# A memory quarter and a gain vector moved from GpSimd's DMA queue to SyncE's, and later transposes tied to weight slices

## The chip, the cores and the metric

The kernel runs on one NeuronCore of a Trainium2 chip. Its time is the device time of one execution, in microseconds. Of the engines, TensorE (PE) multiplies matrices and transposes tiles by a product with the identity, VectorE (DVE) and ScalarE (ACT) do elementwise work, GpSimd (POOL) does small things, and SyncE (SP) issues transfers. Each engine runs its own list of instructions in order and waits on semaphores. Transfers go through 16 DMA engines; those that SyncE issues are queue q1 of the profile, those that GpSimd issues are q0.

## The reference

One decoder layer on x of 1024 tokens by 2048, and a memory of 256 tokens by 2048:

```python
h = rmsnorm(x, ln_g)
proj = h @ w_in                       # split into the inputs of three groups
# group A: gated MLP over chunks of 128; group B: gated DeltaNet, 8 heads
m = rmsnorm(mem, mem_norm_g)
mk, mv = split(m @ w_mem_kv)          # 2 x 512 columns
p = softmax(cq @ mk^T * 128**-0.5)    # group C: 4 heads, 256 memory tokens
out_c = (p @ mv) * silu(c_z)
y = rmsnorm(x + concat(A, B, C) @ w_out, final_g)
```

The change touches the loading of `mem` and `ln_g` for the first stage, the product `m @ w_mem_kv`, and the preparation of the first tiles of x beside it.

## The kernel before, in words

**Precision.** Every float32 operand of a large product is split into a high part (rounded to the fast format, cast by ScalarE) and a low part (the rest, by VectorE), and a product is three matmuls: high-high, high-low and low-high (`triple`). So each tile costs a cast on ScalarE and a subtraction on VectorE before TensorE can use it.

**The planner.** The body of the kernel does not issue instructions. Each call adds an operation to a `Plan`, with a class (`rank`), its data dependences and, inside `behind(op)`, one more dependence on `op`. `Plan.issue` then runs a list schedule over all engines, with a price for each operation, and emits the instructions in the order of the starts that it finds. The `behind` dependence exists in this planning alone: it moves an instruction in its engine's list, and no semaphore is made for it. Semaphores follow the data and the reuse of buffers. Because all orders come out of one schedule, a changed dependence can move instructions on every engine for some distance behind it.

**The memory K/V stage.** It opens the kernel. `w_mem_kv` comes as 16 slices of 128 rows by 1024 columns (`load_kv(k)`, 0.5 MB each; the first in two halves), into four buffers (two named wraw, two ut), so a slice can be issued when the low part of the slice four before it has been made. Memory has two row tiles of 128 tokens, held in tiles named kT and qT, each in four quarters of 512 columns (`load_mem(q)`: two transfers of 256 KB). `spread_mem(q)` transposes a quarter on TensorE, four 128x128 blocks per row tile into one of two PSUM banks, and splits it into gt (high) and inv (low). Quarter q serves slices 4q to 4q+3. For a slice, ScalarE makes whi (the weights times the norm's gain, cast), VectorE makes wlo, and TensorE adds 12 products of 256 columns into the four banks acc (the keys) and 6 of 512 columns into two banks dn (the values). There are two whi and two wlo buffers, so the cast of a slice waits for TensorE's last use two slices before. `kvmark[k]` is the last product of slice k.

**x beside it.** The first four tiles of x (128 tokens each, four pieces of 512 columns; tiles named vs, kd, then kT and qT again) are prepared inside this stage by `prep`: four squares with a sum on ScalarE (written to jk), the inverse root on GpSimd, a product with that and with ln_g on VectorE (ln_g lies in the four tiles gb, named zg, spread over the partitions by the transfer), a transpose on TensorE, a copy to tn and a cast to ahi on ScalarE, and alo on VectorE. tn is stored to h0d from SyncE. The scale of the memory's rows is found in the same way (squares of kT and qT) and applied at the stage's end, when VectorE empties acc into xr. The next stage, the large projection by `w_in`, then takes over the acc banks.

**Queues before.** SyncE's list opens with the first quarter, slices 0 to 3, then quarters 2 and 3 (counted from 0), then slices as buffers come free, mixed with the tiles of x. A semaphore is shared by every eighth transfer of SyncE, so a transfer waits until the one eight before it has landed. GpSimd issues the second quarter first of all (1.31 and 2.04 us) and the four spreads of ln_g at 3.71 us, although the code places these behind slice 2, as its list has nothing before them to wait for. In this kernel the transposes of the second quarter are planned with those of the first, and the third and fourth quarters are made available when slices 3 and 7 have been added.

Nearly every instruction bears line 295, where the planner calls it, so the tiles' names tell them apart.

Of the kernel before, what the change touches and what calls it, by code (L numbers as in the profile page):

```python
# [17 lines left out]
P = 128  # L18
# [4 lines left out]
HT = 512  # L23
# [37 lines left out]
class Plan:  # L61
# [27 lines left out]
    @contextmanager  # L89
    def rank(self, cls):  # L90
        old, self.cls = self.cls, cls
        yield
        self.cls = old

    @contextmanager
    def behind(self, op):
        old, self.gate = self.gate, op
        yield
        self.gate = old
# [199 lines left out]
def kernel(  # L299
# [21 lines left out]
    x, mem, w_in, out = x[0], mem[0], w_in[0], out[0]  # L321
# [7 lines left out]
    V, S, G, PE, Q = R.dve, R.act, R.pool, R.pe, R.sp  # L329
    rank, behind = R.rank, R.behind  # L330

    def C(shape, name, dt=F32):
        return sb.tile(list(shape), dt, name=name, tag=name)[:]
# [44 lines left out]
    def tok(ap):  # L378

        return ap.rearrange("p (t c) -> p t c", c=P)  # L380
# [59 lines left out]
    def split_to(hi, lo, src, eng):  # L440
        S.copy(hi, src)
        eng.tensor_tensor(out=lo, in0=src, in1=hi, op=ALU.subtract)
# [20 lines left out]
    def triple(a, l, r, start, stop, cls=9):  # L463

        mm(a, l[0], r[0], start, False, cls)
        mm(a, l[0], r[1], False, False, cls)
        return mm(a, l[1], r[0], False, stop, cls)
# [4 lines left out]
    def row_scale(xq):  # L472

        s = small()
        for c in range(4):
            S.activation(jk, xq[c], AF.Square, accum_out=s[:, c : c + 1])
        V.tensor_reduce(s[:, 4:5], s[:, 0:4], axis=AX.X, op=ALU.add)
        V.tensor_scalar(s[:, 4:5], s[:, 4:5], 1.0 / D, EPS, op0=ALU.mult, op1=ALU.add)
        rsqrt_to(s[:, 5:6], s[:, 4:5])
        return s[:, 5:6]  # L480


    def row_tiles(tag):
        if tag in ("inv", "gt", "ut"):
            return [b[:, i * HT : (i + 1) * HT] for b in (ring[tag](), ring[tag]()) for i in range(2)]
        return [ring[tag]() for _ in range(4)]

    gb = [ring["zg"]() for _ in range(4)]
    kvraw += [ring["ut"]() for _ in range(2)]
    mem_rows = [row_tiles("kT"), row_tiles("qT")]  # L490
    x_rows = {}

    def load_mem(q, queue=Q):
        for mt in range(2):
            queue.dma_start(mem_rows[mt][q], mem[mt * P : (mt + 1) * P, q * HT : (q + 1) * HT])

    def kv_parts(k):
        n = XW if k == 0 else 2 * XW
        return [slice(i, i + n) for i in range(0, 2 * XW, n)]

    def load_kv(k):
        for sl in kv_parts(k):
            Q.dma_start(kvraw[k % 4][:, sl], w_mem_kv[k * P : (k + 1) * P, sl])

    def load_x(tt, tag, after=(None,) * 4):
        x_rows[tt] = row_tiles(tag)
        for c in range(4):
            with behind(after[c] or R.gate):
                Q.dma_start(x_rows[tt][c], x[tt * P : (tt + 1) * P, c * HT : (c + 1) * HT])
# [4 lines left out]
    with rank(2):  # L514
        load_mem(0)
        S.dma_start(mrow, mem_norm_g[0].rearrange("(c p) -> c p", p=P))
        load_mem(1, G)
        for k in range(4):
            load_kv(k)
    with rank(3):  # L520
        load_mem(2)
        load_mem(3)
# [4 lines left out]
    def spare():  # L527
        turn["dn"] = 1 - turn["dn"]
        return flip[turn["dn"]]
# [6 lines left out]
    def spread_mem(q):  # L536
        h, l = (ring[t](F32R).rearrange("p (k n) -> p k n", k=4) for t in ("gt", "inv"))
        for mt in range(2):
            tp = spare()
            for k in range(4):  # L540
                PE.transpose(tp[:, k * P : (k + 1) * P], mem_rows[mt][q][:, k * P : (k + 1) * P], ident)
            sl = slice(mt * P, (mt + 1) * P)
            with rank(2):
                split_to(h[:, :, sl], l[:, :, sl], tok(tp), V)
        return h, l

    def prep(tt, put, bank):

        xq = x_rows[tt]
        r = row_scale(xq)  # L550
        for q in range(NQ):
            V.scalar_tensor_tensor(xq[q], xq[q], r, gb[q], op0=ALU.mult, op1=ALU.mult)
            tp = bank()
            for k in range(4):
                PE.transpose(tp[:, k * P : (k + 1) * P], xq[q][:, k * P : (k + 1) * P], ident)
            put(q, tok(tp))
# [6 lines left out]
    def put0(tt):  # L563
        def put(q, tp):
            t = tok(ring["tn"]())
            with rank(1):
                S.copy(t, tp)
            with rank(2):
                split_to(ahq[q][:, tt], alq[q][:, tt], t, V)
            with rank(6):  # L570
                Q.dma_start(h0_d[4 * q : 4 * q + 4, :, tt * P : (tt + 1) * P].rearrange("k p n -> p k n"), t)

        return put
# [2 lines left out]
    rm = []  # L576
    kvmark = []
    mhl = [spread_mem(0)]
    mhl.append(spread_mem(1))
    for k in range(KT):  # L580
        mh, ml = mhl[k // 4]
        if k >= 4:
            with rank(3):
                load_kv(k)
        hi, lo = kvhi[k % 2], kvlo[k % 2]
        with rank(2):
            for sl in kv_parts(k):
                raw = kvraw[k % 4][:, sl]
                S.activation(hi[:, sl], raw, AF.Copy, scale=gcol[:, k : k + 1])
                V.scalar_tensor_tensor(lo[:, sl], raw, gcol[:, k : k + 1], hi[:, sl], op0=ALU.mult, op1=ALU.subtract)  # L590
        kk = k % 4
        for h in range(NX):
            sl = slice(h * P, (h + 1) * P)
            triple(ka[h][:, :NMEM], (hi[:, sl], lo[:, sl]), (mh[:, kk], ml[:, kk]), k == 0, k == KT - 1)
        for mt in range(2):
            sl = slice(mt * P, (mt + 1) * P)
            triple(va[mt], (mh[:, kk, sl], ml[:, kk, sl]), (hi[:, XW:], lo[:, XW:]), k == 0, k == KT - 1)
        kvmark.append(R.ops[-1])
        if k == 2:
            with rank(2), behind(kvmark[-1]):  # L600
                for c in range(4):
                    G.dma_start(gb[c], ln_g[0, c * HT : (c + 1) * HT].partition_broadcast(P))
        if k in (3, 7):
            mhl.append(spread_mem(k // 4 + 2))
        if k == 1:
            load_x(0, "vs", kvmark[1:2] * 4)
        if k == 4:
            load_x(1, "kd", kvmark[4:5] * 4)
        if k == 5:
            prep(0, put0(0), spare)  # L610
            for mt in range(2):
                rm.append(C([P, 1], f"rm{mt}"))
                V.tensor_copy(rm[mt], row_scale(mem_rows[mt]))
        if k == 7:

            dg, rmb = (ring["E"]()[:, 0:NMEM] for _ in range(2))
            for mt in range(2):
                V.tensor_scalar(dg[:, mt * P : (mt + 1) * P], ident, rm[mt], None, op0=ALU.mult)
            pt = spare()
            PE.matmul(pt[:, 0:NMEM], ones, dg, start=True, stop=True)  # L620
            S.copy(rmb, pt[:, 0:NMEM])
        if k == 9:
            prep(1, put0(1), spare)
            load_x(2, "kT", (kvmark[6], kvmark[7], kvmark[7], kvmark[8]))
        if k == 13:
            load_x(3, "qT", (kvmark[10], kvmark[11], kvmark[11], kvmark[12]))
            with rank(2):
                prep(2, put0(2), spare)
# [1147 lines left out]
```

## Time and profile before

| | us |
|---|---|
| median of 3 runs (lowest, highest) | 1641.31 (1639.71, 1642.66) |
| the profiled execution | 1637.3 |
| its span | 1635.5 |
| TensorE busy | 1611.9 (99%) |
| VectorE, ScalarE, GpSimd busy | 1259.8, 1028.6, 293.0 |
| DMA share of q1 and q0 | 67.8% and 12.0% of 16 engines |

In the profile, PEld is the weight load of TensorE, which overlaps its matmuls; SPq is SyncE's issuing. The idle time in brackets behind a row stands before that row on its engine, with what ended it. Rows of the timeline begin with the start in microseconds and the duration. A matmul's duration includes its way through the array, so consecutive ones overlap; the distance of their starts is what one costs. Rows of stretches give the busy time and the count of instructions of each engine, the granted clock of TensorE, the DMA share and the rate. A DMA share can be slightly above 1.

### The profile page before, as it was taken

How to read it: one execution, taken by the hardware profiler on the slowest of the kernel's cores; microseconds unless marked ns; L12 is line 12 of the kernel's file. 1: busy time of each engine (PE TensorE's matmuls, PEld its weight loads, DVE VectorE, ACT ScalarE, POOL GpSimd, SP SyncE). 2: the span in 40 equal slices, each digit the busy share in tenths (PEclk: the TensorE clock that was granted, in tenths of full speed). 3: DMA queues.
4: the chain of work that ended last, by engine and by line, in shares of the span. 5: the costliest groups of instructions: out<-in, count | busy, mean ns of one | idle time of the engine just before them, and what ended most of it. 6: DMA issues, size and time to landing. Idle time of an engine off the chain costs nothing.

```text
span 1635.5 us, 26085 instructions
## 1 busy us (share of the span) xinstructions
PE 1611.9 (99%) x8562; PEld 1353.5 (83%) x8562; DVE 1259.8 (77%) x2082; ACT 1028.6 (63%) x2223; POOL 293.0 (18%) x488
## 2 busy tenths in 40 slices
PE   7999999999999999999999999999999999999997
PEld 6888888888788888888888888888888888888886
DVE  5856777779866467899999897767768888688875
ACT  6957765765375456888685356765666784344345
POOL 1011320361342110222135015231000000000001
PEclk9999999999999999999999999999999999999999
DMA  8977898899976785689878877878968879688746
GB/s 298 269 212 219 251 295 241 250 306 308 361 244 224 259 289 193 190 303 349 285 242 282 298 230 244 271 249 295 319 218 269 264 230 362 199 269 290 226 143 243
DMA packets 278762, 428.93 MB, mean 262 GB/s; under 512 B 30889, under 2 KB 104162, under 8 KB 278626
## 3 DMA queue, kind: packets, MB, share of 16 engines
q1 hardware_dynamic: 255394, 365.24, 67.8%
q0 software_dynamic: 22624, 60.97, 12.0%
q8 instruction: 67, 1.10, 0.3%
q10 hardware_dynamic: 608, 1.06, 0.2%
q14 instruction: 69, 0.57, 0.1%
HBM read 339.57 MB, written 87.06 MB: 261 GB/s over the span
## 4 chain that ended last, share of the span: by engine, by line
PE 88%; DMA 7%; DVE 2%; issue 1%; ACT 1%; SPq 0%; POOL 0%; POOLq 0%; DVEq 0%; ACTq 0%
PE acc L295 67%; PE dn L295 21%; DMA y<-in_w_in_dram 2%; DMA kT<-in_mem_dram 1%; DMA wraw<-in_w_in_dram 1%; DMA raws<-h0d 1%; DMA kd<-in_w_in_dram 0%; DMA ut<-in_x_dram 0%; DMA el<-vd 0%; DVE wlo L295 0%; DMA gd<-y 0%; SPq L295 0%; DVE y L295 0%; DMA y<-h0d 0%; ACT whi L295 0%
## 5 line engine op out<-in xcount | busy, mean ns | idle before, releaser
L295 PE MATMUL acc<-ahi,whi 128*128 128x512 f32 (+1 forms) x1512 | 535.1, 392 | 1.3 <-ACT whi L295 0.6
L295 PE MATMUL acc<-ahi,wlo 128*128 128x512 f32 (+1 forms) x1144 | 447.5, 391 | 0.2 <-DVE small L295 0.2
L295 PEld LDWEIGHTS acc<-ahi,whi 128*128 128x128 f32 x1512 | 282.8, 188 | 57.0 <-ACT whi L295 1.8
L295 PE MATMUL acc<-alo,whi 128*128 128x512 f32 (+1 forms) x776 | 303.2, 391 | 0.0
L295 PEld LDWEIGHTS acc<-ahi,wlo 128*128 128x128 f32 x1144 | 215.7, 189 | 41.5 <-DVE wlo L295 0.4
L295 ACT CAST whi<-wraw 128x512 fp32r<-128x512 f32 (+1 forms) x167 | 133.8, 803 | 133.3 <-PE acc L295 88.8
L295 DVE TENSOR_TENSOR wlo<-wraw,whi 128x512 fp32r<-128x512 f32 (+1 forms) x167 | 153.2, 918 | 64.5 <-ACT whi L295 58.2
L295 ACT CAST ahi<-raws 128x1024 fp32r<-128x1024 f32 x130 | 136.3, 1048 | 68.4 <-PE acc L295 26.1
L295 PEld LDWEIGHTS acc<-alo,whi 128*128 128x128 f32 x776 | 146.3, 189 | 27.5 <-DVE alo L295 0.2
L295 PE MATMUL acc<-ahi,zl 128*128 128x512 f32 x376 | 149.1, 396 | 0.0
L295 PE MATMUL acc<-ahi,zh 128*128 128x512 f32 x376 | 148.6, 395 | 0.3 <-ACT vs L295 0.3
L295 PE MATMUL acc<-alo,zh 128*128 128x512 f32 x376 | 148.9, 396 | 0.0
L295 POOL TENSOR_TENSOR small<-small,mhalf 128x1 f32<-128x1 f32 x26 | 16.1, 623 | 584.8 <-DVE small L295 584.7
L295 DVE TENSOR_TENSOR ahi<-raws,ahi 128x1024 fp32r<-128x1024 f32 x65 | 79.8, 1228 | 19.0 <-ACT ahi L295 18.8
L295 DVE TENSOR_TENSOR alo<-y,ahi 128x1024 fp32r<-128x1024 f32 x65 | 79.4, 1221 | 18.5 <-ACT ahi L295 18.4
L295 ACT CAST ahi<-y 128x1024 fp32r<-128x1024 f32 x65 | 68.1, 1048 | 38.4 <-PE dn L295 19.2
L295 DVE TENSOR_TENSOR alo<-raws,ahi 128x1024 fp32r<-128x1024 f32 x65 | 79.4, 1221 | 15.3 <-ACT ahi L295 15.2
L295 PEld LDWEIGHTS acc<-ahi,zh 128*128 128x128 f32 x376 | 70.8, 188 | 13.8 <-ACT vs L295 0.6
L295 PEld LDWEIGHTS acc<-alo,zh 128*128 128x128 f32 x376 | 70.8, 188 | 13.4
L295 PEld LDWEIGHTS acc<-ahi,zl 128*128 128x128 f32 x376 | 70.8, 188 | 13.2
L295 PE MATMUL acc<-whi,ahi 128*128 128x512 f32 x232 | 80.2, 392 | 0.0
L295 PE MATMUL dn<-whi,ahi 128*128 128x512 f32 x216 | 74.2, 390 | 0.0
(419 smaller groups left out, 3405.3 us busy)
## 6 DMA issues: line engine op xcount, KB each, us to landing
wraw<-in_w_in_dram SPq DMA_DIRECT2D x268, 256.0 KB, 4.4
raws<-sd SPq DMA_DIRECT2D x150, 256.0 KB, 3.9
y<-in_w_in_dram SPq DMA_DIRECT2D x92, 256.0 KB, 4.3
y<-sd SPq DMA_DIRECT2D x75, 256.0 KB, 3.9
wraw<-in_w_out_dram SPq DMA_DIRECT2D x64, 256.0 KB, 4.4
raws<-h0d SPq DMA_DIRECT2D x54, 256.0 KB, 5.2
y<-in_w_out_dram SPq DMA_DIRECT2D x33, 256.0 KB, 4.3
sd<-zg SPq DMA_DIRECT2D x32, 256.0 KB, 4.6
```

The source lines that it names most:

```text
L295: o.fn(*o.args, **o.kw)
```

## The change

The second quarter (number 1) is loaded by SyncE, behind slices 0 and 1 and ahead of slices 2 and 3; GpSimd no longer issues it. The four spreads of ln_g are issued by SyncE and planned behind slice 3; GpSimd no longer issues them either. Quarters 1, 2 and 3 are transposed behind slices 1, 4 and 8: the operations are added there, and planned behind the last product of that slice.

```diff
-    def load_mem(q, queue=Q):
+    def load_mem(q):
         for mt in range(2):
-            queue.dma_start(mem_rows[mt][q], mem[mt * P : (mt + 1) * P, q * HT : (q + 1) * HT])
+            Q.dma_start(mem_rows[mt][q], mem[mt * P : (mt + 1) * P, q * HT : (q + 1) * HT])
...
-        load_mem(1, G)
         for k in range(4):
             load_kv(k)
+            if k == 1:
+                load_mem(1)
...
     mhl = [spread_mem(0)]
-    mhl.append(spread_mem(1))
     for k in range(KT):
...
-        if k == 2:
+        if k == 3:
             with rank(2), behind(kvmark[-1]):
                 for c in range(4):
-                    G.dma_start(gb[c], ln_g[0, c * HT : (c + 1) * HT].partition_broadcast(P))
-        if k in (3, 7):
-            mhl.append(spread_mem(k // 4 + 2))
+                    Q.dma_start(gb[c], ln_g[0, c * HT : (c + 1) * HT].partition_broadcast(P))
+        if k in (1, 4, 8):
+            with behind(kvmark[-1]):
+                mhl.append(spread_mem(len(mhl)))
```

In the lists that the planner makes of it, counted from the first instruction: TensorE transposes quarter 1 between slices 1 and 2, quarter 2 between slices 4 and 5, quarter 3's kT half inside slice 9 and its qT half behind the first product of slice 12. SyncE issues the spreads of ln_g behind the weights of slice 8, and three of the four pieces of x's third tile and all stores of x's first tile ahead of the weights of slice 13. On ScalarE some squares come earlier: at slice 13, two of x's third tile stand ahead of whi, and at slice 14 whi stands behind two squares of x's third tile, two of its fourth, and the four tn and four ahi of its second tile. On TensorE the two lists of 6714 rows are the same from about row 1161 on.

## The prediction

> **What bounds the kernel now.** I read the page's busy shares and its chain first, then the first 80 us and the rest in stretches.
>
> ```profile
> span 1635.5 us, 26085 instructions
> PE 1611.9 (99%) x8562; PEld 1353.5 (83%) x8562; DVE 1259.8 (77%) x2082; ACT 1028.6 (63%) x2223; POOL 293.0 (18%) x488
> PE 88%; DMA 7%; DVE 2%; issue 1%; ACT 1%; SPq 0%; POOL 0%; POOLq 0%; DVEq 0%; ACTq 0%
> ```
> ```profile
> core 0: us, PE busy (x) PEld busy (x) DVE busy (x) ACT busy (x) POOL busy (x), PEclk, DMA share, GB/s
> 0.00:10.00 10.00, 3.55 (x14) 2.33 (x14) 1.58 (x4) 3.23 (x5) 4.76 (x15) 1.00 0.77 243
> 10.00:20.00 10.00, 7.77 (x45) 7.23 (x46) 5.16 (x6) 3.85 (x5) 0.00 (x0) 1.00 1.03 402
> 20.00:30.00 10.00, 10.00 (x66) 8.99 (x65) 5.15 (x5) 6.90 (x12) 0.00 (x0) 1.00 0.78 270
> 30.00:40.00 10.00, 10.00 (x71) 9.13 (x70) 8.21 (x14) 9.83 (x21) 1.50 (x2) 1.00 0.93 272
> 40.00:50.00 10.00, 10.00 (x69) 9.15 (x68) 7.29 (x13) 9.64 (x19) 0.55 (x1) 1.00 1.04 326
> 50.00:60.00 10.00, 10.00 (x70) 9.08 (x69) 8.15 (x13) 9.79 (x23) 1.05 (x2) 1.00 0.93 294
> 60.00:70.00 10.00, 9.21 (x63) 7.71 (x61) 9.92 (x18) 9.93 (x23) 0.84 (x4) 1.00 0.79 224
> ```
> ```profile
> 75.00:300.00 225.00, 224.78 (x1118) 1.00 0.82 247
> ```
>
> TensorE is the bound: it idles 23.6 us of 1635.5, of which 8.7 lie in the first 20 us, the head of the memory K/V stage. From 30 us to 70 us ScalarE is 96 to 99% busy beside it, so this stage has a second limit close behind. From 75 to 300 us TensorE misses 0.22 us. The changed order of instructions ends near row 1161 of TensorE's 6714, about 300 us in; behind it both kernels issue the same list. So what the first 75 us gain or lose is carried to the end, and I look nowhere else for a size.
>
> ```profile
> 3.71 2.18 POOL L295 DMA_DIRECT2D zg<-in_ln_g_dram  x4
> 4.13 1.11 PE L295 MATMUL dn<-ident,kT 128*128 128x128 f32 x4 [0.18 <-DMA kT<-in_mem_dram]
> 5.44 1.09 PE L295 MATMUL dn<-ident,qT 128*128 128x128 f32 x4 [0.19 <-DMA qT<-in_mem_dram]
> 9.22 1.36 ACT L295 ACTIVATE whi<-wraw,gcol 128x512 fp32r<-128x512 f32 x2 [2.07 <-DMA wraw<-in_w_mem_kv_dram]
> 10.00 0.58 PE L295 MATMUL acc<-gt,whi 128*128 128x256 f32 x1 [0.54 <-ACT whi L295]
> 10.81 0.42 PE L295 MATMUL acc<-inv,whi 128*128 128x256 f32 x1
> 11.02 0.42 PE L295 MATMUL acc<-gt,whi 128*128 128x256 f32 x1
> 11.45 1.05 PE L295 MATMUL dn<-ident,qT 128*128 128x128 f32 x4
> 12.94 0.29 PE L295 MATMUL acc<-gt,whi 128*128 128x256 f32 x1
> 13.07 0.28 PE L295 MATMUL acc<-inv,whi 128*128 128x256 f32 x1
> 17.80 0.64 PE L295 MATMUL dn<-ident,kT 128*128 128x128 f32 x4 [2.23 <-DMA kT<-in_mem_dram]
> 21.03 1.15 ACT L295 ACTIVATE whi<-ut,gcol 128x1024 fp32r<-128x1024 f32 x1 [4.98 <-PE dn L295]
> ```
>
> Two waits for DMA stand there: the first weight half-slice (ScalarE's cast starts at 9.22, TensorE's product at 10.00), and memory's quarter 2, counted from 0 (2.23 us at 17.80, its transposes standing inside slice 1). The last row is ScalarE's hole behind it. Starts of like matmuls are 0.21 us apart at 11 us and 0.13 at 13: the array starts slow, though the clock column says 1.00.
>
> **The change, part by part.** *Queues.* The quarter and ln_g leave POOL's queue (q0) for SyncE's (q1).
>
> ```profile
> q1 hardware_dynamic: 661, 1.79, 52.4%
> q0 software_dynamic: 432, 1.45, 47.7%
> ```
> ```profile
> q1 hardware_dynamic: 928, 2.36, 102.5%
> q0 software_dynamic: 8, 0.02, 1.4%
> ```
> ```profile
> q1 hardware_dynamic: 232, 0.44, 43.9%
> ```
>
> The first pair is the stretch 4 to 13 us, the second 14 to 20, the last row 0 to 4. POOL's 1.57 MB takes half the engines' time while TensorE waits; alone, q1 moves 2.36/6 = 0.39 MB a us. The first weight half-slice is the third 0.26 MB transfer of q1, complete at 0.79 MB. By 4.0 us q1 has 0.44; the other 0.35 at 0.30 (between 0.20 shared and 0.39 alone) take 1.2 us; the first tile's bytes were there 0.8 us before TensorE used it at 4.13. So it lands near 6.0 to 6.6 and not at 9.2. In the new order ScalarE casts that half-slice (0.68), then memory's second row tile (0.55): the first product starts at 7.6. Bounds: 7.2, and 10.0 if q0 was no brake.
>
> *POOL's four issues and two, now SyncE's six.* At the 0.55 us of ln_g's (2.18 for four, above) six are 3.3 us of SyncE.
>
> ```profile
> SPq L295 <- DVE wlo L295: 14.4, 6, 3.8
> ```
>
> In its first 30 us SyncE waits 14.4 us for weight buffers, which hides them: zero, or 3.3 without that cover. The Trainium skill (Trainium Kernel Development and Optimization, Key Constraints) says that queues of SP, ACT and POOL share the same DMA engines, and that issuing from several only saves issue time; taken strictly it speaks against the move, and the sum would be 3.3 us worse. The shares of q0 and q1 agree on the sharing; what matters here is that the order of the bytes changes.
>
> *Transposes.* Quarter 1 moves behind slice 1, quarter 2 behind slice 4, quarter 3 to slices 9 and 12. Slice by slice: one is 12 products at 0.117 and 6 at 0.23, 2.81 us. New path from 7.6: slices 0 to 3, 11.25; slow clock 1.85 (before, the slow rate held from the transposes at 8.4 to some point between 11.2 and 12.9, taken at 12.1; 3.7 us at half rate); quarter 1's two groups 0.85. Slice 4 starts at 21.55; with quarter 2's 0.85, which before had done by then, 22.4 in equal work. Before, it starts by the chain's row at 26.5 (the chain counts ends, some 0.15 later):
>
> ```profile
> 26.62 1.41 PE acc L295 x12
> ```
>
> Gain there: 4.1, in the main the start's 2.4 and the wait's 2.23, less 1.0 for more products at the slow rate. I take 3.8 for small waits at slices 6 to 9. The Trainium skill (TensorE: Matmul & The Clock Gate, Part 1) gives the slow state a free-running window of about 3.4 us; the 3.7 us above agree in size. By that rule the slow stretch could end up to 3.4 us later than I take, and the gain would be up to 1.7 smaller.
>
> *ln_g.* It leaves SyncE behind slice 8's weights, whose buffer is free when slice 4's low parts are made, 21.4; issued by 23.6. The nearest rows for landing are its own on q0, and those of the weights on q1:
>
> ```profile
> DMA to landing us min/median/max: 7.9/9.2/11.0
> ```
> ```profile
> DMA to landing us min/median/max: 4.6/7.7/9.3
> ```
>
> I take 6.5, nearer to the weights as the queue is theirs, so 30; the ends are 28.2 and 34.6. VectorE needs it for x's first tile at 32.0: hidden by 2 us, with a loss of 1 us per us beyond, 2.6 at most.
>
> *ScalarE behind slice 11, the part that costs.*
>
> ```profile
> 35.07 1.26 ACT L295 COPY tn<-dn 128x512 f32<-128x512 f32 x2
> 36.23 1.14 ACT L295 CAST ahi<-tn 128x512 fp32r<-128x512 f32 x2
> 51.82 0.63 ACT L295 ACTIVATE jk<-kT 128x512 bf16<-128x512 f32 x1
> 52.45 1.14 ACT L295 ACTIVATE whi<-wraw,gcol 128x1024 fp32r<-128x1024 f32 x1
> 54.16 1.28 DVE L295 SCALAR_TENSOR_TENSOR wlo<-wraw,gcol,whi 128x1024 fp32r<-128x1024 f32 x1
> 52.00 0.28 PE L295 MATMUL acc<-gt,whi 128*128 128x256 f32 x1
> 67.75 0.39 PE L295 MATMUL acc<-ahi,whi 128*128 128x256 f32 x1 [0.56 <-DVE xr L295]
> ```
>
> A square (jk) takes 0.72 from start to start, tn 0.5, ahi 0.52, a whole whi 1.05, wlo 1.2. Slice 12 starts at 52.00 before; now at 21.55 + 8 x 2.81 + 3.4 of transposes and the scale's product + 0.5 waits = 47.9. There the half of quarter 3 in qT is only now transposed. ScalarE goes: whi of slice 12 ready at 46.5, a square, a copy, two more squares to 48.95, whi of slice 13 to 50.05, quarter 3's cast (gt) to 50.6. TensorE has 1.75 us of other work (dn 0.23, the transposes 0.41, two dn 0.46, x's 0.41, dn 0.23), so it could use that cast at 49.65: 0.95 lost, and 0.2 behind it. Then ScalarE makes four squares, four tn and four ahi (7.0 us) ahead of slice 14's whi, ready at 58.6; TensorE wants it at 57.8: 0.95 lost with the hand-over. VectorE's wlo for it stands behind three alo and the product with ln_g and comes at 61.05: 0.55. The stage ends at 65.7 instead of 67.0. Before, TensorE then waits to 67.75 for VectorE (xr); now xr is done at 65.4. Gain left: 67.75 - 65.7 = 2.05. Cover for all later work is TensorE's dense 75 to 300 us: zero there; its ends are the 0.22 us that is idle, and -1 to +1 for moved transposes.
>
> **Sum.** 3.8 - 0.95 - 0.2 - 0.95 - 0.55 + 0.75 (xr) = 1.9; with the ends stepped out, 2.05; I take 2.0. The profiled span of 1635.5 becomes 1633.5 and its execution's 1637.3 becomes 1635.3; the median of the three runs is 4.0 above the profiled one, so 1641.3 becomes 1639.3, or -0.12%. A measurement of this kernel tells about 0.2%, 3.3 us.
>
> **Rivals.** (A) This forecast, 1639.3; it has the 96 to 99% of ScalarE for it. (B) The waits at slices 12 to 14 do not arise, as ScalarE, freed of the 4.98 us hole, runs further ahead than I step it: 3.8 + 0.75 = 4.55, 1636.8, faster. For it: before, TensorE lost nothing at 96% of ScalarE. (C) Late weight slices, the other side. ln_g's 1.05 MB moves from 4 to 13 us, where TensorE waits anyway, to 22 to 30 us, and 20 to 60 us is already filled to 0.78, 0.93, 1.04 and 0.93. At 0.33 MB a us it asks for 3.2 us; 36.8 of 40 become 40. If weights then land behind their lead of four slices (11.2 us), the head's gain is lost, and 3.2 more with a few tenths of stall: 1645.0, slower. Against it: the quarter of idle at 20 to 30 us, and landings of at most 9.3 against 11.2. (D) q0 is no brake and the half-slice lands at 9.2 as before: 2.4 less, 1641.7, no change.
>
> **How the numbers follow.** A 0.43, B 0.32, C 0.15, D 0.10. Faster 0.32, same A + D 0.53, slower 0.15. The range goes from 1635.8 (B with the start at 7.2 and 0.6 by transposes moved behind 75 us) to 1643.4 (D with 1.7 lost by a late ln_g); outside it lie C and a little of B. A's own range is 1638 to 1641.
>
> **What would show it.** Right: the first product near 7.6 and not 10.00; no 2.23 us wait for kT; q0 empty before 14 us; slice 12 near 48; TensorE waiting for ScalarE's gt and whi near 50 and 58; the next stage's first product near 65.7. Wrong: whi waiting for weights after 25 us (C), no idle between 45 and 65 us (B), the first cast at 9 us (D), or any new wait between 75 and 300 us.

## The result and the profile after

| | before | after |
|---|---|---|
| median of 6 runs each, us (lowest, highest) | 1641.99 (1639.71, 1645.76) | 1633.93 (1632.33, 1636.60) |
| ratio after to before, 95% interval | | 0.9954 [0.9940, 0.9968] |
| the profiled execution, its span | 1637.3, 1635.5 | 1636.6, 1634.8 |

The changed kernel is 8.1 us faster by the medians, 7.5 by the ratio. The forecast was 1639.3 with a range down to 1635.8, so the direction was among its cases and the size was outside. The two profiled executions differ by only 0.7 us: the one of before lies below all six of its timed runs, the one of after is the slowest of its six. So their ends must not be subtracted; what can be compared is how long the same stretch of work takes in each.

First the page's header, busy shares and chain of the changed kernel, then its first 70 us by stretches (engines in the same order as before), then SyncE's queue at 4 to 13 us:

```profile
span 1634.8 us, 26073 instructions
PE 1611.6 (99%) x8562; PEld 1353.0 (83%) x8562; DVE 1259.3 (77%) x2082; ACT 1029.1 (63%) x2223; POOL 292.1 (18%) x482
PE 88%; DMA 7%; ACT 2%; DVE 2%; issue 1%; SPq 0%; POOLq 0%; POOL 0%; ACTq 0%; DVEq 0%
```
```profile
0.00:10.00 10.00, 4.56 (x18) 3.89 (x19) 2.81 (x5) 4.45 (x6) 1.36 (x9) 1.00 0.74 236
10.00:20.00 10.00, 10.00 (x61) 9.07 (x61) 5.05 (x5) 3.98 (x6) 0.00 (x0) 1.00 1.00 365
20.00:30.00 10.00, 10.00 (x68) 8.85 (x67) 5.46 (x7) 8.62 (x20) 0.55 (x1) 1.00 0.97 327
30.00:40.00 10.00, 10.00 (x72) 9.24 (x71) 8.52 (x14) 9.94 (x20) 0.93 (x1) 1.00 0.96 331
40.00:50.00 10.00, 10.00 (x65) 8.71 (x63) 7.47 (x15) 9.88 (x21) 1.10 (x2) 1.00 1.02 334
50.00:60.00 10.00, 9.17 (x63) 7.43 (x62) 8.72 (x16) 8.94 (x22) 1.34 (x4) 1.00 1.01 300
60.00:70.00 10.00, 8.81 (x61) 7.78 (x60) 9.59 (x18) 9.61 (x21) 0.92 (x1) 1.00 0.54 145
```
```profile
q1 hardware_dynamic: 1320, 3.19, 99.8%
```

The page cannot tell the kernels apart: the busy times agree to 0.9 us (TensorE's to 0.3) and the chain has the same shares. The stretches show the step that was forecast: TensorE is dense from 10 us on (7.77 of 10 before), and gives part of it back from 50 to 70 us. GpSimd's queue moves nothing in the first 14 us, and SyncE's fills the transfer engines from 4 to 13 us.

TensorE's rows of the opening, in the changed kernel: the first product, the first of slice 4, the four waits behind slice 11, and the first product of the next stage.

```profile
7.67 1.22 PE L295 MATMUL acc<-gt,whi 128*128 128x256 f32 x4 [0.92 <-ACT gt L295]
22.17 0.28 PE L295 MATMUL acc<-gt,whi 128*128 128x256 f32 x1
56.75 0.66 PE L295 MATMUL dn<-ident,kT 128*128 128x128 f32 x4 [0.23 <-ACT tn L295]
58.84 0.38 PE L295 MATMUL acc<-gt,whi 128*128 128x256 f32 x1 [0.60 <-ACT whi L295]
61.12 0.75 PE L295 MATMUL acc<-gt,wlo 128*128 128x256 f32 x4 [0.15 <-DVE wlo L295]
65.89 0.28 PE L295 MATMUL acc<-ahi,whi 128*128 128x256 f32 x1
67.31 0.39 PE L295 MATMUL acc<-ahi,wlo 128*128 128x256 f32 x1 [1.03 <-DVE wlo L295]
```

These are close to the steps on record (7.6, 21.55, whi at 58.6, 65.7). The last row is a wait that I had not stepped. All this is worth less than 2 us against the profile shown (1.6 at 165 us), and it is not where most of the 8 us went.

That place is found by matching ScalarE's instructions by name over the whole span and looking where the distance between the two profiles jumps. It jumps twice far behind the stretch in which the two lists differ, and both jumps stand between the second profiles of the two kernels too, which come below. (The two profiles also differ elsewhere, but there two profiles of one kernel differ as much; "What stays open" has the places.) Four rows of ScalarE mark the two stretches, first before, then after:

```profile
527.00 1.05 ACT L295 CAST whi<-wraw 128x1024 fp32r<-128x1024 f32 x1 [2.68 <-PE acc L295]
546.71 0.75 ACT L295 COPY ut<-dn 64x256 f32<-64x256 f32 x2 [3.06 <-issue]
1084.24 0.63 ACT L295 ACTIVATE y<-y 128x512 f32<-128x512 f32 x1 [0.61 <-DVE y L295]
1110.56 1.28 ACT L295 ACT_TABLE_LOAD   x1
```
```profile
529.90 1.05 ACT L295 CAST whi<-wraw 128x1024 fp32r<-128x1024 f32 x1 [2.68 <-PE acc L295]
545.93 0.75 ACT L295 COPY ut<-dn 64x256 f32<-64x256 f32 x2 [1.80 <-issue]
1084.78 0.63 ACT L295 ACTIVATE y<-y 128x512 f32<-128x512 f32 x1 [0.61 <-DVE y L295]
1109.86 1.28 ACT L295 ACT_TABLE_LOAD   x1
```

The first stretch takes 19.71 us before and 16.03 after, the second 26.32 and 25.08: 3.68 and 1.24, together 4.9 us. What happens in them, from the timeline of GpSimd, ScalarE and TensorE, before and then after:

```profile
525.66 1.11 POOL L295 DMA_DIRECT2D kT<-late  x2 [3.43 <-PE dn L295]
527.70 0.61 POOL L295 DMA_DIRECT2D ut<-udrearly  x1 [0.93 <-PE acc L295]
530.22 1.74 POOL L295 DMA_DIRECT2D ut<-udrearly  x3 [1.91 <-issue]
534.18 1.21 POOL L295 TENSOR_TENSOR hs<-hs,mhalf 128x4 f32<-128x4 f32 x1
535.42 1.28 ACT L295 ACTIVATE vs<-vs,hs 128x128 f32<-128x128 f32 x4 [2.42 <-POOL hs L295]
541.45 1.42 PE L295 MATMUL dn<-tblk,gt 128*128 128x64 f32 x8 [1.29 <-ACT ut L295]
1084.55 2.35 POOL L295 DMA_DIRECT2D ut<-udrlate  x4 [3.26 <-PE dn L295]
1090.73 0.40 ACT L295 ACTIVATE vs<-vs,hs 128x128 f32<-128x128 f32 x1 [3.01 <-POOL hs L295]
1094.50 2.00 PE L295 MATMUL dn<-ident,vs 128*128 128x128 f32 x8
```
```profile
528.56 1.10 POOL L295 DMA_DIRECT2D kT<-late  x2 [3.23 <-PE dn L295]
530.60 2.34 POOL L295 DMA_DIRECT2D ut<-udrearly  x4 [0.94 <-PE acc L295]
535.16 1.04 POOL L295 TENSOR_TENSOR hs<-hs,mhalf 128x4 f32<-128x4 f32 x1
536.24 1.28 ACT L295 ACTIVATE vs<-vs,hs 128x128 f32<-128x128 f32 x4 [0.34 <-POOL hs L295]
542.27 1.08 PE L295 MATMUL dn<-tblk,gt 128*128 128x64 f32 x8
549.94 0.54 POOL L295 DMA_DIRECT2D vs<-late  x1 [2.11 <-issue]
1082.77 2.34 POOL L295 DMA_DIRECT2D ut<-udrlate  x4 [0.94 <-PE dn L295]
1088.95 0.40 ACT L295 ACTIVATE vs<-vs,hs 128x128 f32<-128x128 f32 x1 [0.69 <-POOL hs L295]
1095.04 1.04 PE L295 MATMUL dn<-ident,vs 128*128 128x128 f32 x8
```

And the row of the stretch 500 to 560 us, TensorE's busy time first and its granted clock third from the end, before and then after:

```profile
500.00:560.00 60.00, 58.67 (x343) 49.46 (x342) 33.85 (x53) 31.39 (x73) 11.44 (x19) 0.97 0.72 232
```
```profile
500.00:560.00 60.00, 59.97 (x390) 50.84 (x388) 36.66 (x56) 33.95 (x75) 11.88 (x21) 1.00 0.77 254
```

GpSimd issues a run of transfers there and then computes hs, an inverse root that ScalarE needs. Before, between the first and the second ut it pauses for 1.91 us and waits for nothing that the profile shows ("issue"). Hs is late by that, ScalarE waits 2.42 us for it and not 0.34, TensorE is idle for 1.29 us at 541, and its clock over 500 to 560 is 0.97 and not 1.00. By the starts of TensorE's instructions the 3.68 us are three parts: 0.75 in its transposes of vs, the last five of which follow ScalarE's scaling of vs (starts 0.29 us apart and not 0.11), 1.33 with the idle time, and 1.6 behind it, where starts of like products are 0.43 us apart until 544.5 and not 0.23. After the change the pause still exists, 2.11 us long, but stands at 549.94, between two transfers behind hs, where nothing hangs on it. At 1084 it is the same again: the gap ahead of ut is 3.26 us before and 0.94 after (its label, a wait for TensorE, cannot be the reason for the longer one, as the same wait takes 0.94). ScalarE waits 3.01 us for hs and not 0.69, and TensorE's eight transposes of vs take 2.00 us and not 1.04, again most of them at the pace of the scaling, 0.29 us from start to start. No idle time is shown for TensorE there, as its rows overlap.

So the six transfers that left GpSimd's queue at 1 to 6 us seem to have moved a pause at 528 us. Whether they really did is what the experiments had to show.

### The profile page after: what moved, and what is told of

Read it like the earlier page. It is cut to its first block, busy times and chain, and to the rows that moved or that the text cites. A ratio compares the mean times of both kernels' runs of the same rounds, so it can differ in the third digit from the quotient of the medians.

```text
span 1634.8 us, 26073 instructions
## 1 busy us (share of the span) xinstructions
PE 1611.6 (99%) x8562; PEld 1353.0 (83%) x8562; DVE 1259.3 (77%) x2082; ACT 1029.1 (63%) x2223; POOL 292.1 (18%) x482
## 4 chain that ended last, share of the span: by engine, by line
PE 88%; DMA 7%; ACT 2%; DVE 2%; issue 1%; SPq 0%; POOLq 0%; POOL 0%; ACTq 0%; DVEq 0%
PE acc L295 67%; PE dn L295 20%; DMA y<-in_w_in_dram 1%; DMA wraw<-in_w_in_dram 1%; ACT whi L295 1%; DMA raws<-h0d 1%; DMA ut<-in_x_dram 0%; DVE wlo L295 0%; DMA kd<-in_w_in_dram 0%; ACT jk L295 0%; DMA el<-vd 0%; DMA qT<-in_w_in_dram 0%; DMA kT<-in_w_in_dram 0%; DMA wraw<-in_w_mem_kv_dram 0%; DMA kT<-in_x_dram 0%
```

## The experiments

Each ratio is to the kernel before, timed beside it on the same chip. The first four were made when I still looked for an opening that costs before more in its ordinary executions than in the one profiled (theory O), against a gain by the changed order of the instructions (theory S).

### The two kernels again

No edit.

> The kernel before, unchanged, for a second profile: its first one was of an execution of 1637.3, below all six of its timed ones (1639.7 to 1645.8). Theory O (opening): ordinary executions lose the missing time in the first 75 us, so in an execution of 1641 or more the next stage's first product comes 3 to 6 us later than the 67.75 of the first profile. Theory S (later stretches): that product comes within 1 us of 67.75, and TensorE idles 3 to 6 us more than before in 300 to 450 us and 740 to 800 us, where it waits for transfers. Time: the same as before, within 1.5 us.

> The changed kernel, unchanged, for a second profile: its first one was of the slowest of its six executions (1636.6, the others 1632.3 to 1634.6). Theory O: opening as in the first profile (next stage's first product at 65.9), and the time 6 to 9 us below the kernel before because that one is late in the opening. Theory S: opening the same too, but 2 to 4 us less idle time of TensorE in 300 to 450 us and 740 to 800 us than in the first profile when the execution is a fast one.

Measured: before again 1641.92, ratio 1.0001 [0.9988, 1.0014]; after again 1632.87, ratio 0.9945 [0.9927, 0.9964]. The difference holds. The four marks take 20.01 and 26.32 us in the one and 16.04 and 25.07 in the other, as in the first two profiles. The second profile of before opens faster than the first: ScalarE's instructions come some 1.8 us earlier in it from 60 to 360 us (0.9 at 250), as much as in the two profiles of the changed kernel (1.6 and 1.8 at 165 us). So theory O falls: it wanted later openings in other executions of before, and this one is earlier, level with the changed kernel's. Of what theory S wanted, the later stretches came in part: the second profile of before loses 2.5 us to the first over 360 to 460 us and 4.4 over 700 to 800.

### The queues alone

```diff
-        load_mem(1, G)
         for k in range(4):
             load_kv(k)
+            if k == 1:
+                load_mem(1)
...
-        if k == 2:
+        if k == 3:
             with rank(2), behind(kvmark[-1]):
                 for c in range(4):
-                    G.dma_start(gb[c], ln_g[0, c * HT : (c + 1) * HT].partition_broadcast(P))
+                    Q.dma_start(gb[c], ln_g[0, c * HT : (c + 1) * HT].partition_broadcast(P))
```

> Both loads in SyncE's queue as in the change, transposes planned as in the kernel before. Theory O: the gain is the queues': 5 to 8 us faster than before, first product near 7.6 us. Theory S (the order of instructions from 75 to 300 us, which only the moved transposes change, decides): 0 to 2 us faster.

Measured: 1633.97, ratio 0.9954 [0.9937, 0.9972], all of the gain. Marks 16.02 and 25.07. The first product starts at 7.43, so time and start are what theory O wanted too; only the profile of before again speaks against its reason. Theory S, which wanted 0 to 2 us, falls.

### The transposes alone

```diff
-    mhl.append(spread_mem(1))
...
-        if k in (3, 7):
-            mhl.append(spread_mem(k // 4 + 2))
+        if k in (1, 4, 8):
+            with behind(kvmark[-1]):
+                mhl.append(spread_mem(len(mhl)))
```

> Transposes of quarters 1, 2 and 3 behind slices 1, 4 and 8 as in the change, both loads from GpSimd as in the kernel before. Theory O: 0 to 2.5 us faster (the 2.23 us wait for quarter 2 goes, the start stays at 10.0). Theory S: 5 to 8 us faster, since it has the changed order of 75 to 300 us.

Measured: 1641.36, ratio 0.9993 [0.9980, 1.0005], none of it beyond the noise. Marks 19.60 and 26.29, with the pause where it was. So the order of the instructions is not the cause. From here on theory G stood: the gain is the place of GpSimd's pause, and the place goes by how much its queue has issued. Its rivals are T, that the moved transfers gain by themselves, each its part, and later I, that idle transfers cost by themselves.

### One of the two loads alone

The quarter alone: the first part of the diff under "The queues alone". ln_g alone: the second part.

> Only memory's second quarter goes to SyncE; ln_g stays with GpSimd, whose queue so issues two transfers fewer than in the kernel before. Theory G (the gain is a pause of some 1.9 us in GpSimd's own issuing, whose place goes by how much its queue has issued; in the kernel before it stands between the first and the second ut<-udrearly at 528 us, and the inverse root hs at 534 is late by it): two transfers fewer move the pause by two or three transfers, to the third or fourth ut<-udrearly or to kd, all still ahead of hs, so the 3.8 us stay lost; 1638 to 1642.5, ratio 0.998 to 1.0005. Theory T (the gain is a sum of what the transfers themselves cost): a third of the gain, ratio 0.9985, and a pause no longer ahead of hs isn't needed for it.

> Only ln_g's four spreads go to SyncE: four GpSimd transfers fewer. Theory G: the pause moves four to seven transfers later than in the kernel before: if it lands ahead of hs (at kd, qT, ai or qT of 532 to 534 us) the kernel is as slow as before, 1638 to 1642.5; if it lands behind hs (kd or ai of 535, or vs of 546) TensorE's idle 1.3 us at 541 is gone and the kernel is at 1633.5 to 1637.5. In both cases the time goes with the place of the pause, which the trace shows. Theory T: two thirds of the gain whatever the place, 1636 to 1637.5, ratio 0.9967.

Measured: the quarter alone 1640.39, ratio 0.9995 [0.9981, 1.0009]; ln_g alone 1632.22, ratio 0.9935 [0.9916, 0.9953]. Not a third and two thirds, but nothing and everything. The interval of the first still holds T's third (0.9985), but that of the second leaves out its two thirds (0.9967), and the marks show none of the gain in the first stretch for the one and all of it for the other. In the first, the pause has moved five transfers on and is still ahead of hs, which comes at 534.40; its marks are 19.71 and 25.52. In the second there is no pause between kT and hs; marks 16.04 and 25.07. GpSimd's row with the quarter alone:

```profile
533.27 0.54 POOL L295 DMA_DIRECT2D ai<-late  x1 [1.66 <-issue]
```

### Six idle transfers put back

The changed kernel, with six transfers of the constant tile of ones (64 KB each) from GpSimd to a buffer that nobody reads, near 100 us. The lists of all other engines are as in the changed kernel.

```diff
     decays(0, a)
+    with rank(6), behind(marks[-1]):
+        for i in range(6):
+            G.dma_start(DT([P, P], f"idle{i}"), ones)
```

> The changed kernel with six idle transfers more in GpSimd's queue (the constant tile of ones, 64 KB each, to a DRAM buffer that nobody reads), issued behind the decay products, near 100 us; every other engine's list is as in the changed kernel. Theory G: the pause is back near 528 us or anywhere ahead of hs, TensorE is idle for 1.3 us again at about 541, clock 0.97 in 500 to 560; 3.5 to 4.5 us slower than the changed kernel, 1636.5 to 1639, ratio to the kernel before 0.9965 to 0.9985. Theory T (queues' load in the opening): no difference from the changed kernel, 1632 to 1635, ratio 0.9945 to 0.996.

Measured: 1639.03, ratio 0.9985 [0.9974, 0.9996]: 5.1 us slower than the changed kernel's first median, 6.2 slower than its second, a little more than the 3.5 to 4.5 expected. Rows of the timeline, and the stretch 500 to 560:

```profile
534.92 1.75 POOL L295 DMA_DIRECT2D ut<-udrearly  x3 [1.90 <-issue]
540.13 1.28 ACT L295 ACTIVATE vs<-vs,hs 128x128 f32<-128x128 f32 x4 [2.42 <-POOL hs L295]
546.16 1.08 PE L295 MATMUL dn<-tblk,gt 128*128 128x64 f32 x8 [1.30 <-ACT ut L295]
```
```profile
500.00:560.00 60.00, 58.66 (x371) 49.23 (x370) 33.70 (x52) 31.95 (x73) 12.06 (x21) 0.97 0.73 239
```

The opening is the changed one, and the stretch is that of before to the hundredth: the pause between the first and the second ut, 1.90 us, the wait of 2.42, the idle 1.30, the clock 0.97, the marks 19.71 and 26.33. Six transfers fewer and six idle ones more make the same count and the same place. The bytes and packets are not the same: the six that left were 1.57 MB in 480 packets, the six idle ones are 0.39 MB in 192. So the place goes by how many transfers, or instructions, stand ahead in GpSimd's list, and not by what they move.

### Idle transfers added to the kernel before

The same lines in the kernel before, with six and with twelve.

> The kernel before with the same six idle transfers more in GpSimd's queue near 100 us; every other engine's list is as in the kernel before. Theory G: the pause comes some six transfers earlier, to the vs<-late of 494 or the ut<-udrearly of 521, which have 20 us of slack; TensorE isn't idle at 541; 3 to 4 us faster than the kernel before although it does more: 1637.5 to 1639.5, ratio 0.9973 to 0.9985. If it lands on kT<-late of 526 it stays slow. Theory T: the same as the kernel before or up to 1 us slower, ratio 1 to 1.0008.

> The kernel before with twelve idle transfers more in GpSimd's queue near 100 us. Theory G: the pause leaves the stretch between kT<-late and hs towards earlier transfers (vs<-late of 494 or ut<-udrearly of 521, with slack); where the trace shows it there, TensorE is dense at 541 and the kernel is 3.5 to 5 us faster than before, 1636.5 to 1638.5; where the trace shows it still behind kT<-late, as slow as before. Theory I: 5 to 11 us slower than before, or at the least no faster.

Measured: with six 1640.66, ratio 0.9993 [0.9981, 1.0005]; with twelve 1637.69, ratio 0.9972 [0.9959, 0.9985]. With six the expectation missed the place: the pause moved by one transfer only, to the gap between kT and the first ut (first row), still ahead of hs, and nothing was gained; marks 19.77 and 25.34. With twelve it is gone from there. The wait ahead of the ut of 522 is 23.95 us and not 21.67, so the pause now lies within a wait that is there anyway; the marks are 16.06 and 25.08. A kernel that does twelve transfers more for nothing is 4.3 us faster. GpSimd's row with six, and then GpSimd's, ScalarE's and TensorE's with twelve:

```profile
529.01 2.36 POOL L295 DMA_DIRECT2D ut<-udrearly  x4 [3.07 <-PE dn L295]
```
```profile
522.65 1.12 POOL L295 DMA_DIRECT2D ut<-udrearly  x2 [23.95 <-PE dn L295]
527.20 2.36 POOL L295 DMA_DIRECT2D ut<-udrearly  x4 [0.93 <-PE acc L295]
532.87 1.29 ACT L295 ACTIVATE vs<-vs,hs 128x128 f32<-128x128 f32 x4 [0.35 <-POOL hs L295]
538.91 1.08 PE L295 MATMUL dn<-tblk,gt 128*128 128x64 f32 x8
```

The row of the kernel before that answers to the first of these:

```profile
520.88 1.12 POOL L295 DMA_DIRECT2D ut<-udrearly  x2 [21.67 <-PE dn L295]
```

### Two and four idle transfers, and six from SyncE

The same lines in the changed kernel with two and with four; then six with `Q.dma_start` in place of `G.dma_start`.

> The changed kernel with two idle transfers more in GpSimd's queue near 100 us, every other engine's list unchanged. Theory G (where GpSimd's pause falls goes by the number of transfers that its queue has issued, and the time goes by whether the pause stands between the kT<-late of 525 us and the inverse root hs): the queue has issued four fewer than in the kernel before, as with ln_g alone moved, where no pause stood there. TensorE dense at 541, clock 1.00 in 500 to 560, time as the changed kernel, 1632 to 1635. Theory I (idle transfers cost by themselves, some 0.9 us each): 1634.5 to 1636.

> The changed kernel with four idle transfers more. Theory G: two fewer than in the kernel before, as with the memory quarter alone moved: the pause between the qT<-late and the ai<-late ahead of hs, TensorE idle some 1.3 us at 541 and clock 0.97 in 500 to 560; the second pause ahead of the kd<-late of 1089; 1637 to 1640. Theory I: 1636 to 1638 and no pause ahead of hs.

> The changed kernel with the same six idle transfers issued by SyncE instead of GpSimd, GpSimd's list as in the changed kernel. Theory G: GpSimd's queue has issued as many as in the changed kernel, so its pauses stand where they stood, TensorE is dense at 541: 1632 to 1635.5, with up to 1 us for the transfers themselves in SyncE's queue. Theory I: as slow as the same six in GpSimd's queue, 1638 to 1640.

Measured: two 1635.52, ratio 0.9967 [0.9952, 0.9981]; four 1638.61, ratio 0.9984 [0.9974, 0.9995]; six from SyncE 1634.54, ratio 0.9963 [0.9951, 0.9975]. With four, GpSimd has issued as many as with the quarter alone moved, and the pause is ahead of the same transfer with the same length (first row). TensorE's idle 1.30 is there too (second row), but its clock over 500 to 560 is 1.00 and not 0.97, and the first stretch takes 18.14 us and not 19.71. Starts of like products behind the idle time are 0.23 us apart here, and 0.43 with the quarter alone. So of the 3.7 us, 2.1 are the late hs and 1.6 come with the slower clock, which does not follow every time.

```profile
534.30 0.54 POOL L295 DMA_DIRECT2D ai<-late  x1 [1.66 <-issue]
542.95 1.08 PE L295 MATMUL dn<-tblk,gt 128*128 128x64 f32 x8 [1.30 <-ACT ut L295]
```

With two the count is that of ln_g alone moved, and there is no pause between kT and hs, as there; the median is 1.6 to 2.7 us above the changed kernel's two and 0.5 above what was expected, though the marks are 16.06 and 25.08. It lies within theory I's 1634.5 to 1636, so two idle transfers may cost something by themselves; what speaks against theory I as the whole account are the twelve, which made a kernel faster. With six from SyncE the pause stands where the changed kernel has it, ahead of the second vs (548.33, 2.11 us), and the time is within 0.6 us of the changed kernel's. So what costs is that the idle transfers stand in GpSimd's queue, not their traffic.

All kernels by GpSimd's transfers ahead of 500 us against before (the last columns are the two marked stretches and the median of the timed runs):

| transfers | kernel | pause of 526 to 550 us | stretch 1 | stretch 2 | median |
|---|---|---|---|---|---|
| +12 | before, twelve idle | in the wait ahead of ut, 522 us | 16.06 | 25.08 | 1637.69 |
| +6 | before, six idle | kT, then ut | 19.77 | 25.34 | 1640.66 |
| 0 | before | ut 1, then ut 2 | 19.71 | 26.32 | 1641.99 |
| 0 | before again | ut 1, then ut 2 | 20.01 | 26.32 | 1641.92 |
| 0 | transposes alone | ut 1, then ut 2 | 19.60 | 26.29 | 1641.36 |
| 0 | after, six idle | ut 1, then ut 2 | 19.71 | 26.33 | 1639.03 |
| -2 | quarter alone | qT, then ai | 19.71 | 25.52 | 1640.39 |
| -2 | after, four idle | qT, then ai | 18.14 | 25.55 | 1638.61 |
| -4 | ln_g alone | none ahead of hs | 16.04 | 25.07 | 1632.22 |
| -4 | after, two idle | none ahead of hs | 16.06 | 25.08 | 1635.52 |
| -6 | after | vs 1, then vs 2, behind hs | 16.03 | 25.08 | 1633.93 |
| -6 | after again | vs 1, then vs 2, behind hs | 16.04 | 25.07 | 1632.87 |
| -6 | queues alone | vs 1, then vs 2, behind hs | 16.02 | 25.07 | 1633.97 |
| -6 | after, six from SyncE | vs 1, then vs 2, behind hs | 16.04 | 25.08 | 1634.54 |

Every kernel with the pause ahead of hs is at 1638.6 or above, every one without it at 1637.7 or below; the two nearest of these, 1638.61 and 1637.69, are not told apart by their times. Counted in GpSimd's own list, the pause stands ahead of its 170th transfer at 0, the 173rd at -2, the 174th at -6, the 175th at +6 and the 177th at +12: it stays within eight places of the list, while the number of transfers ahead of the work changes by 18.

## Why the prediction was wrong

**The step that failed** is the bound on where to look: "behind it both kernels issue the same list. So what the first 75 us gain or lose is carried to the end, and I look nowhere else for a size", and with it "Cover for all later work is TensorE's dense 75 to 300 us: zero there". The lists are the same from row 1161 on, but an engine's time for the same list was not: GpSimd's pause stands at another instruction of it when fewer transfers went before. The cover that the forecast took as zero is by the marks 3.68 + 1.24 = 4.9 of the 7.5 us; put back by idle transfers it cost 5.1 to 6.2, taken away from the kernel before by idle transfers it gave 4.3. The row was in the trace of before (530.22, 1.91 of "issue", then TensorE's 1.29 idle), in a stretch that I had not opened.

**The queue that lost the issues** was the blind side. I priced the six issues on the queue that gets them ("zero, or 3.3 without that cover"), and on the one that loses them only as traffic. On SyncE zero was nearly right: the opening, stepped with zero for them, ended within 0.2 us of the step, and six idle transfers more there, near 100 us, made 0.6 to 1.7 us between medians, with intervals that overlap, and not 3.3. The strict reading of the Trainium skill (Trainium Kernel Development and Optimization, Key Constraints) that I set beside it, 3.3 worse, did not come. On GpSimd the size of the whole change was in its own list.

**The opening** came as stepped: first product 7.67 for 7.6, no wait for kT, GpSimd's queue empty, slice 4 at 22.17 for 21.55, waits for whi and wlo behind slice 11 of 0.60 and 0.15 (0.95 and 0.55 on record), and 65.89 for 65.7. Slice 4's 0.6 is the slow rate: starts of products of 256 columns are 0.21 us apart until 11.25 and 0.12 from 12.85, those of 512 columns between them still 0.43 until 12.53 (0.23 later). So it held some 1.2 us longer than the 3.7 us from 7.6 that I took. I had also read its end in the kernel before too early: starts are 0.21 apart there until 12.94, and I took 12.1, so the 3.7 us were 4.5. The 1.7 that the rule of the Trainium skill (TensorE: Matmul & The Clock Gate, Part 1) allowed was not used up. The 0.95 and 0.2 at slice 12 did not come (no wait stands between 47 and 56 us); not stepped was VectorE's wlo at 67.31, 1.03 us.

**What these 2 us were counted from** was weaker than I said. "The start's 2.4" is 10.00 less 7.6, and 10.00 is one execution: the second profile of before has 7.76, with no edit, and the transposes alone, with the old queues, 9.10. Between profiles of one kernel the opening varies by about as much as the whole forecast gain. In the timed runs, with the pause back at its old place, the changed kernel is 2.8 us faster than before, six idle transfers included (1641.8 to 1639.0; by the interval 0.7 to 4.3). That is the size of the forecast, and it would fit rival A. But the profiles show only some 0.4 us of it at 165 us (mean of ScalarE's xr copy in the four executions with the opening of before, and in the six with the changed one), so where the rest of it comes from stays open.

**Rivals.** B, the one on the faster side, reached 1636.8 by leaving out the waits at slices 12 to 14. Those at slice 12 stayed out, those behind it came; the time was below B for another reason. C did not come: TensorE is dense from 10 to 50 us. D did not come in the changed kernel (its cast starts at 6.42), though the second profile of before shows that its 7.76 needs no change of queues.

**What stays open.** Why GpSimd pauses: its rows say "issue" and no more. A transfer of instructions (q14) stands near 529 us in before, but at the same point of ScalarE's list in kernels without the pause, so it is not shown to be the cause. The place follows the count, in the order of the table and exactly for equal counts, but not in proportion: six more move it by one transfer, two fewer by five. At -4 no pause is seen there at all; it may lie in GpSimd's wait of 8 to 9 us ahead of vs. No run tells the number of transfers from the number of GpSimd's instructions. Of the second stretch's 1.24 us, 0.9 lie in TensorE's transposes of vs; the rest is spread. Between 360 and 460 us the two profiles of the changed kernel drift apart by 4.4 us, and between 700 and 800 us those of before by as much, which is why single profiles cannot be compared by their ends.

## What to carry to other kernels

When a transfer leaves a queue, price the queue that it leaves over the whole span: list that engine's later rows with "issue" of about 2 us, and ask what stands behind each and has no slack, since the pause may move on or off it. Compare two profiles by the length of the same stretch between two named instructions, not by their ends, and take a second profile of the kernel before a start is used as a term. A suspected count can be tested without touching the rest, by idle work in that queue alone.

## What the runs showed of the hardware that I had not expected

GpSimd's issuing of transfers pauses, at a few places in 1.6 ms, for 1.4 to 2.3 us while it waits for nothing shown, and where it does near 530 us depends on how many transfers its list has ahead: equal counts gave the same instruction and nearly the same length (1.90 or 1.91 in four executions, 1.66 in two, 2.11 to 2.26 in four). The same pause of 1.66 us on a path without slack cost 3.7 with the quarter alone, where TensorE's clock over 500 to 560 was 0.97 behind the idle 1.3 us, and 2.1 with four idle transfers, where it was 1.00. Twelve useless transfers made a kernel 4.3 us faster.
